# Another simulator behind the list scheduler of an encoder trunk in one program

## The chip, the core and the metric

The kernel runs on one core of one Trainium2 chip. A core has five engines with an instruction stream each: TensorE (PE, matrix products; its weight loads are listed apart as PEld), VectorE (DVE), ScalarE (ACT), GpSimd (POOL) and SyncE (SP, which here only issues DMAs). Each engine runs its own stream in the order in which the program has it, and waits on semaphores for the others. The metric is the device time of one execution, in microseconds (us).

## What is computed

The reference is a two-layer encoder on 512 tokens of width 1024, in float32. Each layer is a token mixer and a squared-ReLU MLP, both with a residual and a layer norm:

```python
for i in range(DEPTH):                 # DEPTH = 2
    m = _mixer_gdn(x, ...) if i % 2 == 0 else _mixer_gla(x, ...)
    x = _layernorm(DEEPNORM_ALPHA * x + m, ln1_g[i], ln1_b[i])
    x = _layernorm(DEEPNORM_ALPHA * x + _sq_relu_mlp(x, mlp_w1[i], mlp_w2[i]), ln2_g[i], ln2_b[i])
```

`_mixer_gdn` is the gated DeltaNet (GDN): a projection to q, k, v, z and gates, a short convolution and silu on q, k, v, then in both directions a chunked recurrence with a triangular solve, 8 heads of 128; a norm, a gate and an output projection follow. `_mixer_gla` is gated linear attention (GLA) with 4 heads, also in both directions. The MLP is `relu(h @ w1)**2 @ w2` with 4096 hidden features.

## The kernel before

The four stages follow each other: `gdn`, `mlp`, `gla`, `mlp`. All large products are made of three: each float32 operand is split into a high part in a reduced format and the rest (`split`, line 80: an ACT copy at line 90 for `wh`, a DVE subtraction at line 91 for `wl`), and `mm3` (lines 109 to 111) adds high x high, high x low, low x high in PSUM. A product of a 128x128 block with 512 columns is thus three matmuls of 512 columns.

**Weights** come in blocks of 512 KB through `wcols` and `wrows`, whose DMAs SP issues (line 45) into the pool `wst` of three buffers; the split parts go to `wh` and `wl`, three buffers each. A block can be loaded when its buffer has been split, and split when its `wh`, `wl` are free.

**GDN** goes over the heads as a pipeline of three (`gdn`): for each `i` it traces `recur` of head `i-2` (the recurrence: matmuls `m`, then `op`), `solve` of head `i-1` (the triangular solve: `kk`, `ep`, `hp`, `xp`, ten steps `lv`, then `nw`, each followed by a DVE or ACT operation that the next one needs), `project` of head `i` (four projections `pjk`, `pjq`, `pjv`, `pjz` of 24 matmuls each, then the convolution into the tile `sil`), `rows` of head `i`, and at last `finish` of head `i-2` (norm, `otp` transposes, `p`). `sil` has three buffers, so three heads can be in flight. The generators' yields once told a planner how long a step takes; here they are simply run to their end:

```python
def run(*gens):
    for gen in gens:
        for _ in gen:
            pass
...
if old:
    run(old.recur(done))
if mid:
    run(mid.solve(done))
if new:
    run(new.project(done), new.rows(done))
...
if old:
    run(old.finish(done))
```

**What sets the order.** The text is traced once, in the order written. On leaving the `TileContext` the compiler orders the instructions. Its list scheduler drives a simulated core: where an engine can take an instruction, it gets the ready one that was written first. So an instruction written later can go ahead of one whose inputs the simulation takes as not there yet. Buffers of a pool are handed out in that order as well, and semaphores are put in afterwards. In GDN nothing else fixes the order: the scheduler mixes the projections of one head with the solve and recurrence of the others.

Some orders are fixed by the text, whatever the simulation says. `in_order` (line 53) chains the PE instructions of GLA's heads in the order written, which there is interleaved by hand with `behind`. `issue_after` puts the reload of the exp and ln table (`exp_ln_after`, line 47) behind a silu on ACT, and the first weight splits behind the transposes of `x`.

**The MLP** works in four groups of 1024 hidden features. For a group, `feature` (a projection `pj` with w1, then relu and square, lines 276 and 277) makes `h`, and `second` multiplies with w2 by a scheme of seven products on half blocks (`pX`, `pY`, `pZ`), which needs sums of w2 blocks; POOL makes these by accumulating DMAs (line 303, `plus`). w2 blocks (`w2r`, ten buffers) come on SP's queue along with the w1 blocks. `last` is the last group with the layer norm; at the end SP writes the output.

## Time and profile before

| | us |
|---|---|
| median of 3 runs | 1401.55 |
| lowest, highest | 1400.87, 1402.34 |
| the profiled execution | 1402.67 |
| its span, first to last instruction | 1401.0 |
| mean granted TensorE clock in it | 0.996 of full |

The profile is of one execution. Its page gives busy time for each engine; the other views answer for a stretch of the span, a line of the program or a tile. A matmul's recorded time runs from its first read to a modelled end and overlaps with the next one's: what a matmul costs PE in a full stretch is read from the distance between starts. A row of the timeline such as `x8` is a merged run of eight instructions. The arrow in brackets behind a row names what ended the engine's idle time ahead of it. In the windows view one row is one stretch with the busy time of each engine in it.

### The profile page before, as it was taken

Reading aid. Unit: us, or ns where it says so; the run is one execution under the profiler, and the core shown is the slowest. Engines: PE = TensorE matmul, PEld = TensorE weight load, DVE = VectorE, ACT = ScalarE, POOL = GpSimd, SP = SyncE. Lnnn points to the kernel's source line nnn. Section 1 sums busy time; section 2 is a strip of 40 time slices with the busy share of each in tenths; the row PEclk is TensorE's granted clock in tenths of the full one; section 3 lists DMA queues with packets and bytes.
Section 4 is the critical chain, followed back from the end, with each engine's and each line's share of the span. In section 5 each row is a group of like instructions: output and inputs, shape, how many; then the busy total and the mean of one; then the engine's idle time right before and its main releaser. Section 6 shows DMA issues by size and latency. Waiting matters only on the chain.

```text
span 1401.0 us, 20210 instructions
## 1 busy us (share of the span) xinstructions
PE 1363.1 (97%) x7917; PEld 1117.2 (80%) x7917; DVE 929.5 (66%) x1539; ACT 689.9 (49%) x1320; POOL 122.2 (9%) x169
## 2 busy tenths in 40 slices
PE   7999999999999999999999999999999999999997
PEld 6777777777777888888887888888869788888886
DVE  5787787778667365655555577977773555656655
ACT  3776657665633454444443254554433544445430
POOL 5000000000003300100000100000011000001000
PEclk9999999999999999999999999999999999999999
DMA  6312111211133964655422232221218566646121
GB/s 171 76 48 60 47 46 46 61 46 46 47 108 93 295 153 149 143 157 120 105 91 56 82 91 76 61 64 58 91 46 249 152 185 150 165 121 134 48 80 55
DMA packets 154198, 142.62 MB, mean 102 GB/s; under 512 B 9503, under 2 KB 124311, under 8 KB 154103
## 3 DMA queue, kind: packets, MB, share of 16 engines
q1 hardware_dynamic: 145280, 111.89, 26.7%
q0 software_dynamic: 8256, 29.37, 10.8%
q8 instruction: 62, 1.02, 0.3%
q14 instruction: 33, 0.27, 0.1%
q10 hardware_dynamic: 567, 0.08, 0.0%
HBM read 114.05 MB, written 2.10 MB: 83 GB/s over the span
## 4 chain that ended last, share of the span: by engine, by line
PE 58%; issue 23%; DMA 7%; ACT 6%; DVE 3%; POOL 3%; SPq 0%; POOLq 0%; DVEq 0%; ACTq 0%
DMA w2r<-w2r 4%; PE pj L109 4%; PE pj L110 4%; PE pj L111 4%; PE pjv L109 3%; PE pjv L111 3%; PE pjv L110 3%; PE scp L689 2%; PE op L1346 2%; PE pjq L110 1%; DMA wst<-in_mlp_w 1%; PE pjq L111 1%; PE pjq L109 1%; PE op L777 1%; PE lv L1221 1%
## 5 line engine op out<-in xcount | busy, mean ns | idle before, releaser
L91 DVE TENSOR_TENSOR wl<-wst,wh 128x1024 fp32r<-128x1024 f32 x137 | 168.7, 1232 | 197.7 <-ACT wh L90 196.9
L90 ACT CAST wh<-wst 128x1024 fp32r<-128x1024 f32 x137 | 144.0, 1051 | 283.3 <-PE pj L110 174.5
L109 PE MATMUL pj<-xth,wh 128*128 128x512 f32 (+1 forms) x544 | 202.7, 373 | 3.9 <-ACT h L276 3.2
L111 PE MATMUL pj<-xth,wl 128*128 128x512 f32 (+1 forms) x544 | 202.2, 372 | 0.5 <-DVE wl L91 0.5
L110 PE MATMUL pj<-xtl,wh 128*128 128x512 f32 (+1 forms) x544 | 202.1, 372 | 0.4 <-DVE xtl L150 0.4
L91 DVE TENSOR_TENSOR w2l<-w2r,w2h 128x1024 fp32r<-128x1024 f32 x84 | 102.6, 1221 | 69.3 <-ACT w2h L90 69.3
L109 PEld LDWEIGHTS pj<-xth,wh 128*128 128x128 f32 x544 | 102.6, 189 | 22.8 <-ACT h L276 4.5
L111 PEld LDWEIGHTS pj<-xth,wl 128*128 128x128 f32 x544 | 102.6, 189 | 19.0 <-DVE wl L91 1.0
L110 PEld LDWEIGHTS pj<-xtl,wh 128*128 128x128 f32 x544 | 102.9, 189 | 18.6 <-DVE xtl L150 0.8
L90 ACT CAST w2h<-w2r 128x1024 fp32r<-128x1024 f32 x84 | 88.2, 1050 | 58.2 <-DMA w2r<-in_mlp_w 25.6
L303 POOL DMA_DIRECT2D w2r<-w2r x48 | 41.5, 902 | 402.9 <-DVE w2l L91 235.7
L90 ACT CAST ah<-h 128x1024 fp32r<-128x1024 f32 x40 | 42.2, 1054 | 41.1 <-PE pX L110 16.8
L110 PE MATMUL pX<-w2l,ah 128*128 128x512 f32 x144 | 56.1, 390 | 0.0
L109 PE MATMUL pX<-w2h,ah 128*128 128x512 f32 x144 | 56.1, 390 | 0.0
L111 PE MATMUL pX<-w2h,al 128*128 128x512 f32 x144 | 56.1, 390 | 0.0
L109 PE MATMUL pjv<-wh,xth 128*128 128x512 f32 x128 | 54.7, 428 | 0.0
L91 DVE TENSOR_TENSOR al<-h,ah 128x1024 fp32r<-128x1024 f32 x40 | 48.9, 1222 | 5.7 <-ACT ah L90 4.2
L160 ACT ACTIVATE rsy<-rsv 128x1 f32<-128x1 f32 (+1 forms) x28 | 5.6, 201 | 90.9 <-DVE rsv L159 90.9
L111 PE MATMUL pjv<-wh,xtl 128*128 128x512 f32 x128 | 50.2, 392 | 0.0
L110 PE MATMUL pjv<-wl,xth 128*128 128x512 f32 x128 | 49.9, 390 | 0.0
L1169 POOL TENSOR_TENSOR atl<-on,ath 128x512 f16<-128x512 f32 x16 | 20.9, 1308 | 323.2 <-ACT ath L1168 171.5
L109 PE MATMUL pjk<-xth,wh 128*128 128x512 f32 (+1 forms) x112 | 42.0, 375 | 0.5 <-ACT wh L90 0.5
(434 smaller groups left out, 3440.5 us busy)
## 6 DMA issues: line engine op xcount, KB each, us to landing
wst<-in_mlp_w SPq DMA_DIRECT2D x80, 512.0 KB, 4.1
w2r<-in_mlp_w SPq DMA_DIRECT2D x48, 512.0 KB, 4.4
w2r<-w2r POOLq DMA_DIRECT2D x48, 512.0 KB, 5.7
wst<-in_a_w_in SPq DMA_DIRECT2D x32, 512.0 KB, 4.0
wst<-in_b_w_in SPq DMA_DIRECT2D x32, 256.0 KB, 3.1
wst<-in_a_w_out SPq DMA_DIRECT2D x8, 512.0 KB, 3.8
wst<-in_b_w_in SPq DMA_DIRECT2D x8, 512.0 KB, 3.8
wst<-in_b_w_out SPq DMA_DIRECT2D x8, 512.0 KB, 3.6
```

The costliest lines, as they stand in the source:

```text
L90: nc.scalar.copy(hi, src)
L91: nc.vector.tensor_tensor(lo, src, hi.bitcast(F32), ALU.subtract)
L109: mm(ps, ah, bh, start=start, stop=False, **kw)
L110: mm(ps, ah, bl, start=False, stop=False, **kw)
L111: mm(ps, al, bh, start=False, stop=stop, **kw)
L160: nc.scalar.activation(y, v, AF.Ln)
L303: nc.gpsimd.dma_start(blocks[a + (q,)], blocks[b + (q,)], accum_op=ALU.add)
L689: T.matmul(ps[:, n, :], kh[:, sl], qh[:, sl], start=True, stop=True)
L777: T.matmul(ops, l, r, start=i == 0, stop=i == len(mm) - 1)
L1169: G.tensor_tensor(atl[:, us, :], at, ath[:, us, :], ALU.subtract)
L1221: T.matmul(ps[:, u, :, :], lhs[:, u, :], cols(rhs, u, s, i), start=True, stop=True)
L1346: T.matmul(op[:, n, :], l, r, start=i == 0, stop=i == len(mm) - 1)
```

## The change

One argument is added where the kernel opens the compiler's context:

```diff
-    with tile.TileContext(nc) as tc:
+    with tile.TileContext(nc, schedule_with_timeline_sim=True) as tc:
         body(tc, nc, aps, out)
```

With it the same list scheduler drives another simulator: one that holds a timeline of events for each instruction on its engine, sequencer and queues, in place of the plain simulator with one cost for each instruction. Which instruction counts as ready when, and when an engine can take one, may come out differently, and so may the order on every engine, SP's and POOL's DMA issues included, and which buffer a tile gets. The operations that the text asks for, their shapes, the pools and their numbers of buffers, and the orders that the text fixes stay as they are.

## The prediction

> **What bounds the kernel now.** I read the page's head first, for the busiest engine.
>
> ```profile
> span 1401.0 us, 20210 instructions
> PE 1363.1 (97%) x7917; PEld 1117.2 (80%) x7917; DVE 929.5 (66%) x1539; ACT 689.9 (49%) x1320; POOL 122.2 (9%) x169
> ```
>
> TensorE (PE) is busy for all but 38 us; the next engine, VectorE (DVE), is at 66%. So an order of instructions can only gain where PE is not working. The second view cuts the span into the kernel's stages: gated DeltaNet (GDN) with its loads, its end and the first layer norm, the first MLP, its end, gated linear attention (GLA), its end, the second MLP, the tail. Columns: stretch, its length, then busy us and instructions of PE, PEld, DVE, ACT, POOL, the granted clock, the DMA share and GB/s.
>
> ```profile
> 0.00:50.00 50.00, 41.95 (x242) 35.83 (x243) 30.17 (x58) 23.85 (x42) 18.21 (x47) 1.00 0.56 152
> 50.00:400.00 350.00, 343.82 (x2959) 270.04 (x2958) 276.61 (x602) 222.70 (x630) 22.80 (x19) 1.00 0.19 52
> 400.00:460.00 60.00, 55.63 (x332) 44.80 (x332) 41.71 (x89) 24.06 (x57) 15.34 (x20) 1.00 0.39 122
> 460.00:750.00 290.00, 288.87 (x1294) 237.88 (x1293) 166.14 (x170) 138.15 (x164) 26.06 (x38) 1.00 0.58 147
> 750.00:830.00 80.00, 75.68 (x423) 63.91 (x422) 48.36 (x88) 27.52 (x45) 9.16 (x10) 1.00 0.23 67
> 830.00:1010.00 180.00, 180.00 (x935) 153.65 (x934) 142.26 (x246) 91.55 (x170) 2.86 (x3) 1.00 0.23 69
> 1010.00:1095.00 85.00, 80.01 (x435) 65.69 (x434) 45.05 (x79) 34.63 (x62) 10.65 (x12) 0.98 0.56 161
> 1095.00:1352.00 257.00, 257.00 (x1134) 212.52 (x1133) 149.94 (x151) 123.60 (x144) 17.16 (x20) 1.00 0.51 129
> 1352.00:1401.00 49.00, 40.11 (x177) 32.85 (x175) 29.25 (x60) 3.89 (x11) 0.00 (x0) 0.93 0.11 43
> ```
>
> Both MLPs are full: 257 us hold 1134 matmuls, 226.6 ns each, with no idle time. No order can better that price; it can only spoil it. GLA is full too, and its PE order is pinned by the text (`in_order`). The start (8 us idle) is the first load; the tail (9 us) is the last layer norm and the write. What is left is GDN: 350 us, 6.2 us of them idle by the record. But a recorded matmul (390 ns and more) is longer than its spacing, so waits hide inside "busy". The timeline of PE over one head's period shows them; columns are start, us, engine, line, operation, tiles, count.
>
> ```profile
> 254.49 0.48 PE L109 MATMUL pjk<-xth,wh 128*128 128x512 f32 x1
> 254.81 0.39 PE L110 MATMUL pjk<-xtl,wh 128*128 128x512 f32 x1
> 255.04 0.40 PE L111 MATMUL pjk<-xth,wl 128*128 128x512 f32 x1
> ...
> 257.22 0.41 PE L1221 MATMUL lv<-pz,Xd 128*128 128x64 f16 x8
> 257.47 0.40 PE L1221 MATMUL lv<-Xd,pz 128*128 128x64 f16 x8
> ...
> 259.76 0.39 PE L109 MATMUL pjk<-xth,wh 128*128 128x512 f32 x1
> 260.21 0.28 PE L1221 MATMUL lv<-pz,Xd 128*128 128x64 f16 x4
> 260.76 0.28 PE L1221 MATMUL lv<-pz,Xd 128*128 128x64 f16 x4 [0.27 <-ACT pz L1235]
> 260.87 0.40 PE L1221 MATMUL lv<-Xd,pz 128*128 128x64 f16 x8
> 261.11 0.47 PE L110 MATMUL pjk<-xtl,wh 128*128 128x512 f32 x1
> ...
> 265.47 0.22 PE L1263 MATMUL nw<-Dd,ath 128*128 128x128 f16 x1
> 265.52 0.22 PE L1264 MATMUL nw<-Dd,atl 128*128 128x128 f16 x1
> ...
> 273.10 0.60 PE L1369 MATMUL otp<-ident,fo 128*128 128x128 f32 x4
> ...
> 273.76 1.06 PE L1142 MATMUL kk<-sil 128*128 128x128 f32 x8
> 274.65 0.46 PE L1321 MATMUL m<-vt,xf 128*128 128x128 f32 x2
> ...
> 281.83 0.40 PE L111 MATMUL pjv<-xth,wl 128*128 128x512 f32 x1
> 282.48 0.49 PE L1321 MATMUL m<-r,xf 128*128 128x128 f32 x2 [0.26 <-DVE r L1315]
> ```
>
> Two things are to be seen. The projections of the next head (`pjk`, `pjv`) fill the time between the steps of the chain of the heads before (`lv`, `m`, `nw`). And PE stands still before a chain step whose input is late, although a projection matmul, needing nothing new, comes right after it: after 259.76 PE should be free at 259.99, four `lv` need 0.12 us, yet the next four start at 260.76: 0.65 us lost, while `pjk` runs on at 261.11. Likewise 281.83 to 282.48: 0.65 for a matmul of 0.23, 0.42 lost, with `pjv` to follow.
>
> **The change, part by part.** It removes no operation and adds none in the text. It moves potentially every instruction in its own engine's stream; buffers are handed out in that order too. So I cost it by stage.
>
> GDN. The chain of waits gives the length of a head: the activation table of each head's silu is loaded once.
>
> ```profile
> 118.02 1.28 ACT L1066
> ...
> 242.31 3.39 PE op L1346 x28
> ...
> 345.21 1.28 ACT L1066
> ```
>
> Five heads lie between the outer rows: (345.21 - 118.02)/5 = 45.44 us a head. What PE must do in it, by counts from the code and spacings of the rows above: 96 projection matmuls at 0.2266 make 21.8; 120 `lv` at 0.031 (257.22 to 257.47 for 8) 3.7; 100 float matmuls of 128 columns at 0.111 (273.76 to 274.65 for 8) 11.1; 36 half-precision ones of 128 columns at 0.055 (265.47 to 265.52) 2.0; 4 of 512 columns 0.9; 24 small `hp` at 0.03 0.7. Sum 40.2. So 5.2 us a head are not work. Part is the change of shape: a projection after another shape takes 0.32 (254.49 to 254.81) instead of 0.23, and this timeline has 29 such, recorded as 0.47 us and longer: 2.6 us, which any interleaving pays. The other 2.6 us are waits, 21 us for eight heads. That is the upper bound of the gain here; the lower bound of what exists is the 6.2 us of recorded idle time.
>
> A simulator that knows better when an input lands puts one or two projections more before the late step. It gains where such a filler is at hand, as in both places quoted: 0.65 + 0.42 = 1.1 us a head, 8.6 for eight heads. I take **9 us**, nearer to that row than to either bound. Against it stands at most what finer interleaving adds: one more return per wait at 0.09.
>
> The chain itself is kept from going late by slack: `op` of a head ends at 245.70, yet its `otp` (the last part, written after the next head's projections) starts at 273.10, 27.4 us later. That covers a chain that gets longer; once it is used up, the next head's buffer (`sil`, three of them) comes late, and PE starves.
>
> DVE (277 of 350 us) and ACT (223) have no room for long mistakes, but 2.6 us of lateness in a head falls under the same slack. ACT's table loads (1.28 us) could double if an exp slips between a silu and its reload; at 64% ACT hides one more pair a head.
>
> Stage ends. The costliest single stop in the kernel is at the start of the second MLP (timeline, all engines):
>
> ```profile
> 1087.98 0.39 PE L111 MATMUL pj<-xth,wl 128*128 128x512 f32 x1
> ...
> 1089.37 1.04 ACT L90 CAST wh<-wst 128x1024 fp32r<-128x1024 f32 x1 [2.21 <-DMA wst<-in_mlp_w]
> ...
> 1090.96 0.80 PE L109 MATMUL pj<-xth,wh 128*128 128x512 f32 x1 [2.59 <-ACT h L276]
> ...
> 1091.56 0.63 PE L110 MATMUL pj<-xtl,wh 128*128 128x512 f32 x1
> ...
> 1091.98 0.63 PE L111 MATMUL pj<-xth,wl 128*128 128x512 f32 x1
> ```
> ```profile
> 1090.00:1095.00 5.00, 4.04 (x12) 3.25 (x13) 2.45 (x2) 3.71 (x6) 0.00 (x0) 0.66 1.03 298
> ```
>
> A w1 block lands late behind w2 blocks in SP's queue at 298 GB/s; PE stands 2.75 us, then runs at a granted clock of 0.66 over these 5 us (0.42 a matmul), about 1.7 us more: 4.5 us in all. An order that knows the queue's load can run another matmul there, but the DMAs, free to go as soon as a buffer is, will still crowd. I take 2 of the 4.5; bounds 0 and 4.5. POOL is at 9% and its `w2r` sums are needed late; moves there cost nothing until PE waits for one.
>
> MLPs and GLA: 0, hidden by nothing since PE is full; they are the downside below.
>
> **Sum.** The profiled execution took 1402.67 us (span 1401.0 and 1.67 around it); less 9 and 2 it is 1391.7. It stood 1.1 above the median of the runs, 1401.55, so I predict 1390.6, rounded **1391 us**.
>
> [...]
>
> **The rivals.** First, *queues fill too early* (slower). If the simulator lets an engine's queue take what is ready before the engine is free, projections enter ahead of the chain step that becomes ready a moment later. A head's chain visits PE some 30 times (18 in `solve`, 11 in `recur`, 1 in `finish`). The slack of 27.4 us covers 0.9 us a visit, four projection matmuls. From the fifth on, each costs 30 x 0.2266 / 3 = 2.3 us a head (three heads in flight), 18 us in all: 1401.55 + 18 = **1420**. For it: the chain steps sit between as few as three projections now. Against it: the waits quoted have too few, not too many. [...]
>
> Second, *a full stage gets a hole* (slower). The two MLPs have six boundaries between groups, where w2 halves, their sums on POOL and the splits must be ready together. One stop like that at 1088 in each is 6 x 4.5 = 27; in half of them 13: **1415**. [...]
>
> Third, *much the same*: PE is full, and gains in one head are lost in another: **1401**.
>
> Fourth, *all waits go*: 21 in GDN, 4 at 1088: 1401.55 - 25 = **1377**.
>
> **How the numbers follow.** Forecast 0.38, all waits go 0.09, much the same 0.15, queues fill 0.24, a hole 0.14. Hence faster by over 0.2% (2.8 us, about what a measurement of this kernel can tell) 0.47, within it 0.15, slower 0.38. Faster cases alone would span 1377 to 1398; the range for 8 in 10 goes from 1377 to 1428, the first rival with a little more than one filler too many (1.5 x 18 = 27).
>
> **What would show it.** In the new profile: the head's period (silu to silu) 44.3 instead of 45.44 us, with as many 0.47 us returns; PE in 50 to 400 us with fewer named waits; no 2.6 us stop at the second MLP's start. The first rival would show a longer period, PE idle behind `sil` conversions and `otp` close after `op`; the second, idle PE inside 460 to 750 or 1095 to 1352. A period unchanged with a different order would mean that waits moved, not went.

## The result

| | before | after |
|---|---|---|
| median, us | 1401.94 (4 runs, 1400.87 to 1403.23) | 1521.58 (4 runs, 1518.67 to 1522.36) |
| ratio after/before, 95% interval | | 1.0851 (1.0835 to 1.0867) |
| span of the profiled execution, us | 1401.0 | 1517.0 |
| mean granted TensorE clock in it | 0.996 | 0.956 |

The change makes the kernel 8.5% slower. The forecast was 1391 us, with a range up to 1428: wrong in sign, and outside the range. The head of the page of after:

```profile
span 1517.0 us, 20179 instructions
PE 1408.1 (93%) x7917; PEld 1171.7 (77%) x7917; DVE 931.1 (61%) x1539; ACT 698.6 (46%) x1320; POOL 123.9 (8%) x169
```

The five rows count as many instructions as before, so the work is the same and its order differs. PE is "busy" for 45 us more with the same 7917 matmuls, at a mean granted clock of 0.956 in place of 0.996. The windows of after, cut at its own stages (columns as in the prediction):

```profile
50.00:500.00 450.00, 387.52 (x2981) 320.78 (x2980) 281.93 (x608) 231.07 (x631) 22.84 (x18) 0.89 0.15 43
500.00:575.00 75.00, 56.20 (x286) 44.29 (x285) 39.40 (x85) 20.62 (x52) 19.14 (x26) 0.84 0.42 120
575.00:865.00 290.00, 288.34 (x1304) 238.91 (x1304) 164.26 (x167) 139.80 (x166) 22.46 (x33) 1.00 0.54 137
...
945.00:1125.00 180.00, 180.00 (x937) 153.79 (x935) 142.14 (x245) 91.75 (x170) 2.86 (x3) 1.00 0.22 68
...
1210.00:1467.00 257.00, 255.84 (x1129) 211.53 (x1128) 151.81 (x152) 126.30 (x148) 17.18 (x20) 1.00 0.53 134
```

The MLPs (third and fifth row) and GLA (fourth) hold the same work in the same time as before. GDN needs 450 us for what took 350, at a granted clock of 0.89, and its end 75 in place of 60. The view by line gives the same cut with first and last start; of before:

```profile
L1346 PE MATMUL op<-vn,qke x128: 272/275/377, 110.8 to 414.1; 128*128 128x128 f32 x128
L1066 ACT ACT_TABLE_LOAD  x8: 1283/1283/1283, 49.0 to 345.2; - x8
```

and of after:

```profile
L1346 PE MATMUL op<-vn,qke x128: 275/275/356, 144.8 to 519.7; 128*128 128x128 f32 x128
L1066 ACT ACT_TABLE_LOAD  x8: 1283/1283/1283, 43.7 to 412.3; - x8
```

The last `op` of the eight heads starts 105.6 us later (519.7 against 414.1); what follows it takes 997.3 us in place of 986.9. So 105.6 of the 116 us are lost in the heads and some 10 in GDN's end. The second row of each is the one table load per head: (412.3 - 43.7)/7 = 52.7 us between heads, before 42.3. This mean of seven intervals is the **period** in the table further down. It takes in the first heads, whose intervals are shorter or longer than the rest, so it ranks the runs only roughly. The last four intervals alone are 45 to 46 us before and 57 to 61 after; the expectations go by these. Of the 105.6 us, 72 lie between the first and the last load; behind the last load 38 more pass until the last `op` than before, and the first load comes 5 earlier.

One such head of after, on PE (timeline):

```profile
285.96 0.80 PE L109 MATMUL pjz<-xth,wh 128*128 128x512 f32 x1
286.55 0.63 PE L110 MATMUL pjz<-xtl,wh 128*128 128x512 f32 x1
286.98 0.63 PE L111 MATMUL pjz<-xth,wl 128*128 128x512 f32 x1
...
302.05 0.24 PE L1180 MATMUL hp<-icc,a 128*128 128x4 f16 x4
...
302.77 0.47 PE L111 MATMUL pjq<-xth,wl 128*128 128x512 f32 x1
...
306.73 0.40 PE L110 MATMUL pjq<-xtl,wh 128*128 128x512 f32 x1
...
307.19 0.17 PE L1180 MATMUL hp<-dc,a 128*128 128x4 f16 x1
...
314.44 0.39 PE L111 MATMUL pjv<-xth,wl 128*128 128x512 f32 x1
...
324.77 0.39 PE L1221 MATMUL lv<-Dd,ath 128*128 128x64 f16 x8 [0.55 <-DVE Dd L1240]
326.36 0.39 PE L1221 MATMUL lv<-pz,Xd 128*128 128x64 f16 x8 [1.20 <-DVE pz L1230]
...
339.67 0.40 PE L1285 MATMUL nw<-Xd,a 128*128 128x128 f16 x4 [2.77 <-DVE qke L1277]
...
344.52 0.80 PE L109 MATMUL pjz<-xth,wh 128*128 128x512 f32 x1
```

From 285.96 to 314.44 lie all the 96 projections, in runs: the step `hp` goes at 302.05, its answer from DVE (`dc`, below) is there at 303.95, but the next `hp` goes at 307.19, behind a run of 18 projections. From there to 344.52, 30 us, there is not one projection; the last steps of the `lv` ladder run bare, and PE waits for DVE or ACT at step after step. DVE in the same head:

```profile
293.15 0.35 DVE L1315 SCALAR_TENSOR_TENSOR r<-m,neg,vt 128x128 f32<-128x128 f32 x1 [4.50 <-PE m L1313]
...
302.63 1.23 DVE L91 TENSOR_TENSOR wl<-wst,wh 128x1024 fp32r<-128x1024 f32 x1 [3.96 <-ACT wh L90]
303.77 0.18 DVE L1182 TENSOR_TENSOR dc<-icc,hp 128x32 f16<-128x32 f16 x1
...
337.68 0.74 DVE L1037 SCALAR_TENSOR_TENSOR sil<-pjv,cw,sil 128x510 f32<-128x510 f32 x1
338.34 1.27 DVE L1277 TENSOR_TENSOR qke<-E,qk 128x512 f32<-128x512 f32 x2
```

While PE works off projections, DVE is idle (4.50, 3.96 us); while the ladder needs DVE, convolutions (`sil`) stand ahead of `qke`, and PE waits 2.8 us for it (339.67 on PE). The engines take turns instead of working side by side. The compiled order of PE's stream shows it as well. Here `so4.7` are the matmuls of step 7 of head 4's `solve`, `re` is `recur`, `ro` is `rows`, `fi` is `finish`, and `[6:9]` are nine projections of head 6 in a row:

```
before  ... so4.5 [5:3] so4.6 [5:9] so4.7 [5:7] so4.8 [5:4] so4.9 [5:1] [6:3] so4.10 [6:6] so4.11
        [6:4] so4.12 ro5.2 [6:1] so4.13 [6:5] so4.14 [6:3] so4.15 [6:2] ro5.3 so4.16 ... fi3.1
after   ... so4.2 [5:18] re3.3 re3.4 so4.3 [5:6] [6:13] re3.4 re3.5 [6:16] so4.4 re3.5 so4.4 ro5.2
        re3.6 ro5.2 [6:18] re3.6 so4.5 re3.7 so4.5 ro5.3 [6:15] re3.7 [6:1] re3.8 so4.6 [6:9] ...
        so4.7 so5.1 ... so4.8 ... so4.12 so4.13 so4.14 so4.15 fi3.1 so4.16 ...
```

In the whole stage before has 180 runs of projections, of 4.1 on average, after 50 of 14.9.

GDN's end is another matter: between the last `op` and the first `pj` of the MLP PE's recorded idle time is 15.9 us, before 1.6. The longest stops are 4.45 us before `otp` at 524.65, 3.54 at 549.13 and 2.99 at 552.75, each behind a step of DVE.

### The profile page after: what moved, and what is told of

It is laid out like the page before. It is cut to its first block, busy times and chain, and to the rows that moved or that the text cites. A ratio compares the mean times of both kernels' runs of the same rounds, so it can differ in the third digit from the quotient of the medians.

```text
span 1517.0 us, 20179 instructions
## 1 busy us (share of the span) xinstructions
PE 1408.1 (93%) x7917; PEld 1171.7 (77%) x7917; DVE 931.1 (61%) x1539; ACT 698.6 (46%) x1320; POOL 123.9 (8%) x169
## 4 chain that ended last, share of the span: by engine, by line
PE 36%; issue 22%; DMA 4%; POOL 2%; DVE 1%; ACT 1%; SPq 0%; DVEq 0%; POOLq 0%; ACTq 0%
PE pj L110 4%; PE pj L111 4%; PE pj L109 4%; DMA w2r<-w2r 2%; PE scp L689 2%; PE pjv L111 2%; PE pjv L109 2%; PE pjv L110 2%; DMA w2r<-in_mlp_w 2%; PE op L777 1%; PE pX L111 1%; PE pX L110 1%; PE pX L109 1%; POOL xt L194 1%; PE pl L110 1%
## 5 line engine op out<-in xcount | busy, mean ns | idle before, releaser
L90 ACT CAST ah<-h 128x1024 fp32r<-128x1024 f32 x40 | 42.2, 1056 | 40.9 <-PE pX L110 16.8
L1169 POOL TENSOR_TENSOR atl<-on,ath 128x512 f16<-128x512 f32 x16 | 21.5, 1346 | 416.9 <-ACT ath L1168 416.9
L1325 ACT ACTIVATE vd<-m,kds 128x128 f32<-128x128 f32 x48 | 17.7, 369 | 58.6 <-PE m L1321 58.4
```

Source lines behind the costliest of these rows:

```text
L90: nc.scalar.copy(hi, src)
L1169: G.tensor_tensor(atl[:, us, :], at, ath[:, us, :], ALU.subtract)
L1325: A.mul(vds[d], m2, self.kds[:, n, d:d + 1])
```

## Experiments

**Theories.** T1: the loss is PE's order in GDN. R: it is the order of ACT and DVE, or which buffer is handed out when. Further theories have letters that the expectations explain. The tool for both is an order held by edges without a semaphore: each instruction of an engine in the stage is tied behind the one that came before it in another program's order. Only the list changes from run to run:

```diff
+    def pinned(self, engine, order):
+        ...
+        for k in order:
+            i = mine[k]
+            if prev is not None:
+                self.tc.add_manual_dep(
+                    i, prev.name, mybir.DependencyInfo(mybir.DependencyClass.NoSync, ...), reason="pinned")
+            prev = i
...
-        gdn(c, ...)
+        with c.pinned(mybir.EngineType.PE, unpack(GDN_PE)):
+            gdn(c, ...)
```

All runs, each against the kernel before on the same chip ("old" and "new" are the plain simulator and the timeline simulator, which order all that is not held):

| run | simulator | median, us | ratio, 95% interval | period, us |
|---|---|---|---|---|
| before | old | 1401 to 1403 | 1 | 42.3 |
| after | new | 1521.58 | 1.0851 (1.0835 to 1.0867) | 52.7 |
| PE of before | new | 1456.85 | 1.0385 (1.0365 to 1.0406) | 49.8 |
| PE of after | old | 1524.94 | 1.0881 (1.0860 to 1.0903) | 52.6 |
| ACT and DVE of before | new | 1574.94 | 1.1238 (1.1216 to 1.1261) | 60.2 |
| PE and DVE of before | new | 1421.54 | 1.0140 (1.0120 to 1.0160) | 44.4 |
| PE, DVE, ACT of before | new | 1407.46 | 1.0046 (1.0029 to 1.0062) | 42.3 |
| projections paced by edges | new | 1570.34 | 1.1214 (1.1187 to 1.1241) | 61.7 |
| bunches of 4 | old | 1423.09 | 1.0144 (1.0128 to 1.0159) | 45.4 |
| bunches of 8 | old | 1447.86 | 1.0322 (1.0303 to 1.0341) | 49.1 |
| bunches of 13 | old | 1487.66 | 1.0612 (1.0579 to 1.0645) | 54.9 |
| after's runs cut at 4 | old | 1564.83 | 1.1162 (1.1140 to 1.1185) | 58.0 |
| 3 per step, rows held back | old | 1547.51 | 1.1033 (1.1013 to 1.1053) | 55.5 |
| 3 and 2 per step | old | 1567.61 | 1.1171 (1.1152 to 1.1190) | 59.1 |
| 3 and 2 per step | new | 1563.61 | 1.1150 (1.1128 to 1.1172) | 58.7 |
| preparation of after, chain of before | old | 1530.57 | 1.0922 (1.0890 to 1.0953) | 61.1 |
| chain of after, preparation of before | old | 1495.16 | 1.0669 (1.0627 to 1.0711) | 47.7 |
| 14 projections moved by the profile | old | 1401.40 | 0.9989 (0.9980 to 0.9998) | 42.2 |

### Which engine's order

PE's order of before under the new simulator, and PE's order of after under the old one:

> The kernel after, with the order of TensorE's 3,049 instructions in the delta-net stage held to the order that they had before; every other engine and stage is ordered as after. Theory T1 (the loss of 116 us sits in TensorE's order in that stage: runs of some 13 ready projections between two steps of the serial solve): the head's period returns to 45 to 46 us and the time to 1400, between 1392 and 1410. Rival R (the loss comes from the orders of ScalarE and VectorE, or from which buffer is handed out when): the period stays over 55 us, the time at 1480 or more.

> The converse: the kernel before, with TensorE's order in the delta-net stage held to the order of the kernel after. T1: the head's period becomes 57 to 60 us and the time about 1505, between 1490 and 1522. R: the period stays at 45 to 48 us, the time at 1425 or less.

The second came out nearly as T1 said: 1524.94, 3 us past its bound, with last intervals of 57 to 60 us; R (1425 or less) falls. Holding PE's order alone costs as much as the whole change. DVE and ACT are free in this run, though, and by its trace DVE's order comes out closer to that of after than to that of before. The first is a miss for both theories: 1456.85, of 120 us 65 come back and 55 stay. The waits of PE in this kernel, from 158 to 392 us (engine, line, what it waited for: us, times, longest):

```profile
PE m L1340 <- DVE r L1334: 10.7, 11, 1.5
PE m L1332 <- DVE sn L1357: 7.5, 7, 1.8
```

The two together are 18 us in some four heads, and before has 0.5 us for `r` in the same stretch and none for `sn`. DVE ahead of one of these waits:

```profile
262.57 0.68 DVE L1170 TENSOR_TENSOR qd<-sil,qd 128x512 f32<-128x512 f32 x1
263.17 0.74 DVE L1056 SCALAR_TENSOR_TENSOR sil<-pjq,cw,sil 128x511 f32<-128x511 f32 x1
263.83 0.68 DVE L1170 TENSOR_TENSOR qd<-sil,qd 128x512 f32<-128x512 f32 x1
264.43 0.60 DVE L1334 SCALAR_TENSOR_TENSOR r<-m,neg,vt 128x128 f32<-128x128 f32 x2
```

`r`, 0.3 us each, on which the recurrence hangs, stands behind convolution and `qd` steps of 0.66 and 0.6 us. It is the pattern seen on PE: ready bulk work ahead of the step that becomes ready a moment later. So DVE was restored too, then ACT:

> As the run with TensorE's order of before, and VectorE's order restored with it; ScalarE's stays with the new simulator. Theory V (VectorE is the second place: it takes ready convolution steps of 0.66 us ahead of the short steps of the recurrence): the 55 us go, 1415 or less, and TensorE's waits for `r` and `sn` with them. Rival A (ScalarE's order, with its exponentials and silu, holds them): 1440 or more.

> The kernel after, with the delta-net stage's orders of TensorE, VectorE and ScalarE all three held to those of before; the DMA queues, GpSimd, the handing out of buffers and all other stages stay with the new simulator. Theory T2 (three orders of one stage that fit each other are the whole cause; the 55 us left with TensorE's order alone restored came from the other two): 1400 us, between 1393 and 1408, period 45 to 46 us. Rival B (buffers, DMA order or other stages hold part of the 55 us): 1425 or more.

With PE's order restored, DVE's is worth 35 us (1456.85 to 1421.54; V had 1415 or less, missed by 7 us); ACT's is worth another 14. With all three restored the time is 1407.46, and the heads run as before (period 42.3, the last `op` at 414). The 5 us left over lie behind them. **The orders of these three engines in this one stage are the cause**; buffers, queues and other stages hold no more than those 5. The converse, ACT and DVE restored with PE left to the simulator:

> The kernel after, with the orders of ScalarE (617 instructions) and VectorE (739) in the delta-net stage held to those of before, and TensorE left to the new simulator. T1: no help, 1480 us or more, and the runs of projections stay long (mean over 8). R: 1400 to 1420 us.

1574.94, worse than after: as T1 said, it does not help (its trace has as many runs of projections up to the last `op` as that of after, 52), and here the mixed orders fit each other worse than either program's own.

### The length of the runs

Here the order of before is kept, except that projections are held back until 13, 8 or 4 are together. The rule that makes the list:

```diff
+for x in order:                    # PE's order of before
+    if is_projection(x):
+        held.append(x)
+        if len(held) >= K: out += held; held = []
+    else:
+        if needs_one_of(held, x): out += held; held = []
+        out.append(x)
```

> The kernel before, where in TensorE's order of the delta-net stage nothing but the place of the projections is changed: they are held back until 13 are together (50 runs of mean 14.9 in the whole stage, as many and as long as in the kernel after; before has 180 of mean 4.1). The other engines are ordered by the plain simulator. T1 (the length of the runs is the cost: some 20 steps of a head lose their cover, 0.7 us each, less 1.9 us of shape returns saved): about 12 us a head, 1480, between 1450 and 1515. Rival L (the length of a run doesn't matter since slack covers it; the mixing of solve and recurrence does): 1395 to 1420.

> As the run with projections held back until 13 are together, but until 8 are together: 78 runs of mean 9.5. T1 (cost follows the length of the runs): between before and 1488, at 1450, from 1430 to 1475. L (the 86 us of the run with 13 come from something else than the length, so a smaller bunch costs about as much): 1480 or more.

> The same with 4: 119 runs of mean 6.3 in place of 180. T1: some eight steps of a head lose their cover, at about 0.5 us, less 0.9 us of shape returns saved: 3 us a head, 1422, from 1405 to 1440. Rival G (before switches shape too often, a little bunching gains): under 1399.

1487.66, 1447.86, 1423.09 for 13, 8 and 4: T1's three figures were 1480, 1450 and 1422, the last two given with the result of 13 known. The table loads of the kernel with 13 (view by line):

```profile
L1085 ACT ACT_TABLE_LOAD  x8: 1283/1283/1283, 49.1 to 433.3; - x8
```

(433.3 - 49.1)/7 = 54.9. The last intervals are 59 to 61 us, so these heads are as slow as those of after. The total stays lower because from the last table load to the start of the last `op` 71 us pass (433.3 to 504.2), before 69 and in after 107, and because what follows takes 985 us, before 987. L and G fall: even runs of 6.3 in place of 4.1 cost 1.4%.

On PE nothing but the place of the projections differs from before, which the traces confirm. DVE and ACT are ordered by the plain simulator, however, and their orders move too, so the cost isn't that of PE's stream alone. PE's waits in the run with 13 (150 to 420 us, some four and a half heads) show where it lies: some 25 us before steps of the solve, 10 before the recurrence, 8 before `ktp`. The reading is that each projection taken into a longer run is cover taken from another step.

### Four cures that did not cure

If the runs cost so much, spreading the projections of after should mend it. First by edges, the projections of the next head tied to the steps of the solve:

```diff
-            if mid:
-                run(mid.solve(done))
+            steps = pe_steps(mid.solve(done)) if mid else []
             if new:
-                run(new.project(done), new.rows(done))
+                fill = [f for step in pe_steps(new.project(done)) for f in step]
+                run(new.rows(done))
+                for j, step in enumerate(steps):
+                    tc.add_manual_dep(fill[j * len(fill) // len(steps)], step[0].name, ..., reason="pace")
```

> The kernel after, with the next head's projections spread over the steps of the current head's solve by ordering edges alone: the share j of the projections may be put on TensorE only behind the first matmul of solve step j. Nothing else is held. T1 (serial solve): the runs of projections in the solve get short, the solve falls from 54 us towards 40, the period to 50 or less and the time to 1445 or less. Rival S (the ring of three silu buffers and of three projection banks sets the period, whatever the solve does): the solve gets shorter but the period stays at 55 us or more, the time at 1490 or more. R: 1490 or more.

1570.34: T1's figure (1445) is missed by far; S has it, a shorter solve (44 us in place of 54) and a longer period. The last projections now come with the end of the solve, so the next head's silu and `rows` come after it: from the first `xf` of one solve to the first `qd` of the next 21.5 us pass (215.94 to 237.40), in after 4.5. By the view of the silu's line, PE waited for it (us, times):

```profile
  PE ktp L1096: 25.1, 6
```

The reading is that the pace was laid over the wrong stretch and made a loop: solve, projections, `rows`, next solve. Then by lists, with the order of after and its projections placed more evenly, in three ways:

```diff
+for x in order:                    # PE's order of after
+    if is_projection(x):           # second run: rows and kk as well
+        held.append(x); continue
+    if is_next_step(x):
+        out += first(held, Q)      # Q = 4; 3; 3 for z and 2 for k, q, v
+    out += all_that(x, needs, held)
+    out.append(x)
```

> The kernel before with TensorE's order of after in the delta-net stage (1525 us as such), but its long runs of projections cut: at most four ahead of each step of the chain, the rest put behind the steps that follow. The order of all other matmuls stays that of after. T1: most of the 124 us goes, 1440 or less. L: 1490 or more.

> A better try at what the run with runs cut at four was to show. The kernel before with TensorE's order of after, at most three projections ahead of each step, and the matmuls of `rows` and of `kk`, which wait for these projections, held back together with them, so that they don't stand in the order ahead of their inputs; 9 of the last steps of the solve stay without a projection. T1 (cover missing for the steps is the cost): 1460, between 1430 and 1485. L (the order of the other matmuls of after is the cost): 1505 or more.

> In the traces of after, of the run with runs cut at four and of the run with three ahead of each step one thing is the same: a head's 96 projections lie in the first half of its period, and 20 to 32 us of chain follow with none. Here TensorE's order of after (1525 us with the plain simulator) has its projections spread over the whole period: three ahead of each step for the last of the four groups, two ahead of each step for the first three of the next head, which then last to the end of the solve. Everything else in the order stays as in after. Theory H (projections and chain one after the other instead of side by side, 29 and 29 us): the stretch without projections falls under 12 us, the period to 52 us or less and the time to 1475 or less. Rival L (the order of the other matmuls of after, or the burst of convolutions on VectorE at a head's start, holds the period): 1505 or more.

> The same order of TensorE under the new simulator, which orders VectorE and ScalarE. H: 1500 or less, but 25 to 50 us above the run with the plain simulator, since the orders of the other two engines cost 14 to 55 us by the earlier runs. L: 1515 or more.

1564.83, 1547.51, 1567.61, 1563.61: all slower than the uncut order. T1 and H were wrong each time, and each time the figure of the rival L was met, which lays the loss on the order of the other matmuls of after, in the third run also on the convolutions that DVE does at a head's start. PE in the third of them:

```profile
308.75 0.60 PE L1167 MATMUL ep<-rt,sel 6*128 6x512 bf16 x1
313.51 0.80 PE L128 MATMUL pjz<-xth,wh 128*128 128x512 f32 x1 [4.16 <-DVE sil L1056]
314.10 0.63 PE L129 MATMUL pjz<-xtl,wh 128*128 128x512 f32 x1
314.53 0.63 PE L130 MATMUL pjz<-xth,wl 128*128 128x512 f32 x1
...
329.34 0.90 PE L1102 MATMUL ktp<-ident,sil 128*128 128x128 f32 x3 [4.24 <-ACT sil L1085]
```

Here the stretch without a projection is down from 30 to some 15 us in the middle heads (H had under 12), but a projection whose bank isn't free yet (`pjz`) and a transpose whose silu isn't done (`ktp`) now stand in the list ahead of chain steps, 4.2 us each, and the projections after them go at 0.43 us (314.10 to 314.53) in place of 0.23. Spreading the projections also made their silu late: in this run PE waited 27.6 us before `ktp` for it, in 6 stops, in the uncut order not at all. So none of these four mended the order, and they leave L standing. They don't say that the runs are harmless, since the spreading brought new waits of its own.

### Which half of PE's order

The last pair exchanges one half each: the place of the next head's preparation (projections, `rows`, `kk`, transposes of v), or the order of the chain (solve, recurrence, finish).

```diff
-order = order_of(before)
+order = chain_of(before) + preparation at the solve steps where after has it     # first run
+order = chain_of(after) + preparation at the solve steps where before has it     # second run
```

> The two halves of TensorE's order of after, one at a time, with the plain simulator. Here the order of the chain (solve, recurrence, finish) is that of before, and the place of the next head's preparation (projections, `rows`, `kk` and the transposes of v) between the solve's steps is that of after, for heads 1 to 5; where a buffer forbids it, 46 matmuls stand a little later. Theory H (the loss is that the preparation lies in one half of the period, and the chain alone in the other): 1480 to 1535, period 54 us or more. Rival L (the order in which solve and recurrence are mixed): 1402 to 1435.

> The other half: the order of the chain of after (solve and recurrence mixed step by step), with the preparation placed as in before, for heads 1 to 5. H: 1402 to 1440 (the last two heads keep the order of after, some 10 to 20 us). L: 1480 or more.

The first is as H said: 1530.57, the place of the preparation alone costs as much as all of PE's order. The second is as L said: 1495.16, where L had 1480 or more and H 1402 to 1440. So both halves cost, and they don't add up (129 + 94 against 123 for both). PE's first wait in the second, 150 to 390 us:

```profile
PE otp L1388 <- DVE fo L1384: 16.3, 4, 4.7
```

4 us a head for `otp`, which stands in the list between solve steps at a point where its input isn't there yet. How much of the chain half is its own cost, and how much such a misfit with the other half, stays open; so it does for the first half.

So this much is shown: the loss is the orders of PE, DVE and ACT in GDN. Holding PE's alone to that of after, with DVE and ACT free to follow, is enough for all of it, and so is the place of the preparation alone; long runs, with PE's order otherwise as before, are enough for 21 to 85 us. How the loss divides between bare steps on PE and the orders that DVE and ACT take beside them stays open: no run holds PE's order of after beside theirs of before. That the new simulator takes a ready projection as soon as a buffer lets it, is read from the order and argued, not shown.

### The term that was to bring the gain

The prediction's gain was one or two projections ahead of each late step. It can be done by hand, from the profile of before:

```diff
+for k in order_of(before):
+    if idle_before(k) >= 0.33 and not is_projection(k):
+        out += next projections behind k, as many as fit       # 12 places, 14 projections
+    out.append(k)
```

> A test of the prediction's own term of 9 us. The kernel before with all three orders of the delta-net stage held as they are, except that ahead of the 12 chain steps for which TensorE stood idle for 0.33 us or more in the profile of before, 14 projections are put that came right behind them. The prediction's term would make it 9 us faster (1393). Counted over the whole stage, though, the waits over 0.3 us are 16, with 8.1 us together, and 14 projections of 0.2266 us are 3.2 us: so 1399, from 1396 to 1403.

1401.40 against 1402.54, a ratio of 0.9989 (0.9980 to 0.9998): 1.1 us gained, not 9, within the bounds of the expectation but less than the 3.2 of its count, and hardly more than the spread lets one tell. At the place that the prediction quotes, one projection went ahead of the late four `lv`:

```profile
259.39 0.28 PE L1240 MATMUL lv<-pz,Xd 128*128 128x64 f16 x4
259.51 0.47 PE L129 MATMUL pjk<-xtl,wh 128*128 128x512 f32 x1
259.94 0.28 PE L1240 MATMUL lv<-pz,Xd 128*128 128x64 f16 x4
```

From one `lv` to the next are 0.55 us, as before (260.21 to 260.76): the filler cost nothing there. At this place the idea works; over the stage it brought little. This version is the only one ahead of both kernels, by a tenth of a per cent.

## Why the prediction was wrong

- **The step that failed** is "a simulator that knows better when an input lands puts one or two projections more before the late step". It put some ten more (50 runs of 14.9 in place of 180 of 4.1), and left the later steps with none. The sign of the forecast hung on this step, and I had inferred the new simulator's decisions from what would be good, not from anything that it showed. The bunches show what each size costs: +21, +45 and +85 us.
- **The slack argument** failed with it. The 27.4 us between `op` and `otp` are slack at the end of a head. The solve has little: before, 7.5 us lie between the first `xf` (269.63) and the next `qd` (277.08). In after the `ep` of the next head (282.43 on PE's timeline) follows the last `nw` of the head before (281.10) directly, and from the first `qd` to the first `xf` a solve of the middle heads takes 54 us (285.45 to 339.53) where it took 38 (231.41 to 269.63). One solve and the 4.5 us to the next `qd` (344.02) make the period of 58.6. Slack has to be read on the chain that recurs in each period.
- **The first rival** had the right mechanism ("queues fill too early") and two of its signs: a longer period, and `otp` close behind `op` (`op` to `p` some 32 us before, 12 after). Its third sign, PE idle behind `sil` conversions, did not show. Its size was wrong, 18 us in place of 116. Its sum lays one filler too many before each of 30 visits, five each, 150 in all, where a head has 96 projections: runs of 14.9 stand before some six visits and leave the others bare. For bare steps it had no term, nor for DVE, whose order is worth 35 us. Its divisor of 3 for "three heads in flight" fails as well, since in after one solve follows the other.
- **The 9 us for GDN** were mis-sized even as a possible gain. The waits are there, 16 over 0.3 us in the stage and 8.1 us together, but the prediction took their whole length for the gain. The 14 projections that were put into 12 of them are 3.2 us of work, and they brought 1.1. "DVE and ACT have no room for long mistakes" was right, and should have had a price.
- **The second MLP's start** gained less than the 2 us forecast, and other stops took that back. Waits of PE ahead of it, in after:

```profile
PE ob L241 <- DVE xt L188: 2.9, 1, 2.9
PE pj L109 <- ACT h L276: 1.2, 1, 1.2
```

In place of the stop of 2.59 us stands one of 1.2, and a new one of 2.9 came up at GLA's end. From the first `pj` on, MLP, GLA and MLP took 368.1, 246.5 and 348.2 us, before 368.9, 244.1 and 349.4: full stages priced at nothing, rightly. The second rival did not occur: no stop inside the two MLP windows is over 1.7 us. The end of GDN, priced at nothing as well, cost 10 us.

## What to carry to other kernels

Where a serial chain runs between filler work, as in GDN here, the fillers must be rationed. Taken early, they delay the step at hand (the next `hp` of after at 307.19 us, its input there at 303.95) and leave later ones bare (30 us without a projection); in bunches of 4, 8 and 13 this cost 21, 45 and 85 us. So look at the length of the filler runs in the compiled order before trusting a scheduler, however well its simulator knows the latencies. An order on several engines is one object: ACT and DVE of before beside PE under the new simulator took 1574.94 us, the preparation of after beside the chain of before 1530.57, both more than the programs that the parts came from. That isn't a rule, since the chain of after beside the preparation of before, 1495.16, lay between.

## What the hardware showed unexpectedly

PE's clock fell without a long stop. Five windows of after, 4 us each, in and just behind the stretch without a projection:

```profile
322.00:326.00 4.00, 2.61 (x39) 2.47 (x39) 1.75 (x4) 1.48 (x8) 0.00 (x0) 1.00 0.00 0
326.00:330.00 4.00, 2.19 (x40) 1.85 (x40) 3.06 (x11) 1.44 (x6) 0.00 (x0) 0.82 0.00 0
330.00:334.00 4.00, 3.34 (x36) 3.00 (x36) 3.01 (x6) 2.32 (x7) 0.00 (x0) 0.50 0.00 0
...
338.00:342.00 4.00, 1.33 (x8) 0.71 (x8) 4.00 (x7) 1.02 (x3) 0.00 (x0) 1.00 0.00 0
342.00:346.00 4.00, 3.41 (x10) 2.22 (x10) 4.00 (x8) 2.43 (x8) 0.00 (x0) 0.52 0.00 0
```

PE's recorded stops from 322 to 330 us are 1.2 us at the longest, yet behind busy shares of 65 and 55% the granted clock goes to 0.50 (330 to 334 us). The prediction quotes 0.66 over the 5 us in which one stop of 2.59 us ended (1090 to 1095). Here the last single stop of that length ended at 281.10, and from 291 to 326 us every window of 4 or 5 us has the clock at 1.00: several short stops came before the fall, no long one. What sets the granted clock, these runs do not show.

The second fall, to 0.52 in the window from 342, stands behind the 2.77 us before `nw` at 339.67 and some shorter stops. It is this kind that the projections pay for: behind the like wait of the head before, 2.78 us at 281.10, ten of them from 286.55 on go at 0.43 us in place of 0.2266, some 2 us, at a granted clock of 0.50 (286 to 291 us).
